# Linear attention on one core: exponentials of the next group before the scores, one tile per direction, and state steps between the groups

## The chip, the core and the metric

One core of a Trainium2 chip runs the whole program. Its engines work side by side, each through its own list of instructions: TensorE (PE in the rows; its weight loads are PEld), VectorE (DVE), ScalarE (ACT), GpSimd (POOL) and SyncE (SP), which issues the loads of weights from memory. The metric is the time of one execution in microseconds (us); it is given as the median of runs. A ratio is the changed kernel's time over the time of the kernel before.

## The reference

Two blocks run one after the other. The first is a trunk of two layers for two streams of 256 tokens, the context `cx` and the latents `x`. In each layer an input projection feeds three mixers: pooling, gated linear attention in both directions (four heads of 64), and softmax attention. Their results go through `w_out`, and a squared-ReLU MLP follows. The factors `sh`, `sc` and `ga` come from one row times `w_mod`. The second block, which the change doesn't touch, has a gated delta rule, dilated attention and two more MLPs.

```python
def gla_chunk_scan(q, k, v, la, s0, strict):
    ...
    mask = np.tril(np.ones((C, C), bool), k=-1 if strict else 0)[:, :, None]

    def step(S, inp):
        qc, kc, vc, lc = inp
        b = jnp.cumsum(lc, axis=2)
        o_inter = jnp.einsum('bhid,bhde->bhie', qc * jnp.exp(b), S)
        diff = b[:, :, :, None, :] - b[:, :, None, :, :]
        decay = jnp.exp(jnp.where(mask, diff, -jnp.inf))
        A = jnp.einsum('bhid,bhjd,bhijd->bhij', qc, kc, decay)
        o = o_inter + jnp.einsum('bhij,bhje->bhie', A, vc)
        bl = b[:, :, -1:, :]
        S_new = jnp.exp(bl[:, :, 0, :, None]) * S + jnp.einsum('bhjd,bhje->bhde', kc * jnp.exp(bl - b), vc)
        return S_new, o
    ...

def gla_bidir(q, k, v, la_f, la_b, s_f, s_b):
    o_f, s_f_new = gla_chunk_scan(q, k, v, la_f, s_f, strict=False)
    rev = lambda a: a[:, ::-1]
    o_b, s_b_new = gla_chunk_scan(rev(q), rev(k), rev(v), rev(la_b), s_b, strict=True)
    return o_f + rev(o_b), s_f_new, s_b_new

def trunk_layer(x, cx, c, c_ctx, ...):
    sh1, sc1, ga1, sh2, sc2, ga2 = modulation(c, w_mod, b_mod)
    ...
    u = (rmsnorm(x, g_mix) * (1 + sc1) + sh1) @ w_in
    uc = (rmsnorm(cx, g_mix) * (1 + sc1c) + sh1c) @ w_in
    ...
    o_gc, s_f, s_b = gla_bidir(*gla_features(gqc, gkc, gvc, rfc, rbc, w_gate, b_gate), s_zero, s_zero)
    o_gl, _, _ = gla_bidir(*gla_features(gq, gk, gv, rf, rb, w_gate, b_gate), s_f, s_b)
    ...
    mix = jnp.concatenate([pool_mixer(...), gla_output(o_gl, ...), latent_attention(ql, k_all, v_all)], axis=-1) @ w_out
    x = x + ga1 * mix
    x = x + ga2 * squared_relu_mlp(rmsnorm(x, g_mlp) * (1 + sc2) + sh2, w_up, w_down)
    ...
```

The latents' scan starts from the states that the context's scan leaves. In layer 1 the context needs only its states.

## The kernel before

The weight projections fill most of TensorE's time. `load_split` (L85) loads a 128x2x512 piece of weights into `raw` (three buffers), and ScalarE and VectorE split it into `hi` (L93) and `lo` (L94); each product is then three matmuls, hi by hi, hi by lo and lo by hi. The pieces of `w_mod` go from `raw` to TensorE without a split, as matmuls of 32x256 with `silu_c` (L407 loads them). Products land in PSUM tiles that belong to a thread: `ps_m` has three buffers, `ps_a` two, `ps_b` two and `ps_o` one. Linear attention works in thread a, and so never has more than two PSUM tiles. Softmax attention works in thread b.

Linear attention takes a stream's heads in pairs. `gla_pair` (L652) makes the decay logarithms `la` (as `la_h` and `la_l`), multiplies them by constant tables `cm` to get sums of logarithms, and takes the exponential on ScalarE (`gla_exp`, L608). Within 128 tokens `gla_intra` (L616) takes the decay between two rows in seven levels of block halves, of 64, 32, 16, 8, 4, 2 and 1 rows, two levels to a group and the last alone. For a group:

- 8 matmuls with `cm` (4 for each direction) make the logarithms, and two exponentials on ScalarE write the group's one tile `E`, which has one buffer for both directions;
- for each level four products on VectorE (L646), of a direction and a kind (q or k), write the tile `lev`;
- for each level four matmuls, each on half the rows of the array (64x128), make the scores of the two heads, head 0 in one `ps_a` tile and head 1 in another; in the trace each of the four is two records;
- two masked copies on VectorE (L649) put them into `at`.

Ahead of the levels stand the state steps (L662 to L685), four in a pair of the context and two in a pair of the latents. Each is a chain over three engines: product `qd` on VectorE (L667), transposition on TensorE (L669), copy `ktt` on ScalarE (L671), matmul on TensorE, and two small updates of the state on VectorE (L681, L683).

Six pairs go through `gla_intra`: two of the context in layer 0, two of the latents in each layer. Two more, of the context in layer 1, make states only.

When the program is built, a scheduler writes out each engine's order from the order of the code and from what each instruction needs; nothing is reordered at run time. Between the instructions of linear attention it puts others that are ready. In the context's two pairs of layer 0 these are matmuls of the input projection (128x512, called fillers in the text). Around the latents' pairs they are the 32x256 matmuls of the pieces of `w_mod` that stream in there, and softmax attention. `w_out` comes after that.

## Time and profile before

| | |
|---|---|
| three runs | 1900.25, 1903.61 and 1904.91 us; the median is 1903.61 us |
| the profiled execution | 1901.48 us, with a span of 1899.4 us inside it |
| mean granted clock of TensorE | 0.994 |
| TensorE busy | 1825.4 us, 96% of the span |
| VectorE, ScalarE busy | 1288.2 us (68%), 1068.3 us (56%) |
| DMA | 307.14 MB, 162 GB/s in the mean |

The span runs from the first instruction of the profiled execution to its last; the time of that execution is 2.1 us more. Busy times overlap between engines, so they don't add up. A matmul's end in a profile is modelled and matmuls are pipelined: the distance from one start to the next tells more than the printed duration.

### The profile page before, as it was taken

How to read it: one execution, taken by the hardware profiler on the slowest of the kernel's cores; microseconds unless marked ns; L12 is line 12 of the kernel's file. 1: busy time of each engine (PE TensorE's matmuls, PEld its weight loads, DVE VectorE, ACT ScalarE, POOL GpSimd, SP SyncE). 2: the span in 40 equal slices, each digit the busy share in tenths (PEclk: the TensorE clock that was granted, in tenths of full speed). 3: DMA queues.
4: the chain of work that ended last, by engine and by line, in shares of the span. 5: the costliest groups of instructions: out<-in, count | busy, mean ns of one | idle time of the engine just before them, and what ended most of it. 6: DMA issues, size and time to landing. Idle time of an engine off the chain costs nothing.

```text
span 1899.4 us, 33154 instructions
## 1 busy us (share of the span) xinstructions
PE 1825.4 (96%) x12272; PEld 1544.8 (81%) x12272; DVE 1288.2 (68%) x2853; ACT 1068.3 (56%) x2080; POOL 59.1 (3%) x60
## 2 busy tenths in 40 slices
PE   7998999999989999999899999998999999999999
PEld 5875567888879998856598889897899987789997
DVE  4465467677777767766566688777766677767665
ACT  5443647755575556646655557453554556675553
POOL 0000000000000000000000000403000000000000
PEclk9999999999999999999999999999999999999999
DMA  7414771355646565466256654131455654435665
GB/s 284 152 46 145 259 257 55 129 187 185 192 131 189 181 195 168 155 198 217 78 168 191 194 173 133 58 101 45 150 187 188 190 175 155 134 112 178 186 191 156
DMA packets 90225, 307.14 MB, mean 162 GB/s; under 512 B 11456, under 2 KB 16096, under 8 KB 90064
## 3 DMA queue, kind: packets, MB, share of 16 engines
q1 hardware_dynamic: 89088, 302.91, 50.1%
q0 software_dynamic: 976, 2.12, 0.3%
q8 instruction: 96, 1.57, 0.3%
q14 instruction: 65, 0.53, 0.1%
HBM read 303.95 MB, written 1.05 MB: 161 GB/s over the span
## 4 chain that ended last, share of the span: by engine, by line
PE 83%; DVE 7%; DMA 4%; ACT 4%; issue 2%; POOL 0%; DVEq 0%; ACTq 0%; POOLq 0%
PE ps_m L76 60%; PE ps_a L76 13%; PE ps_b L76 4%; PE ps_o L76 2%; DMA raw<-in_w_mod_dram 2%; ACT gt L296 1%; DVE k L1202 1%; DVE lo L94 1%; PE ps_b L834 1%; PE ps_b L1215 1%; ACT hh L244 1%; PE ps_m L288 1%; DMA tmpb<-in_band_dram 1%; DMA raw<-in_gdn_w_in_dram 0%; PE ps_m L415 0%
## 5 line engine op out<-in xcount | busy, mean ns | idle before, releaser
L93 ACT CAST hi<-raw 128x512 fp32r<-128x512 f32 (+1 forms) x944 | 576.7, 617 | 533.4 <-PE ps_m L76 288.7
L94 DVE TENSOR_TENSOR lo<-raw,hi 128x512 fp32r<-128x512 f32 (+1 forms) x944 | 636.1, 682 | 330.7 <-PE ps_m L76 203.4
L76 PE MATMUL ps_m<-hh,hi 128*128 128x256 f32 x1440 | 405.4, 282 | 8.9 <-ACT gt L296 4.3
L76 PE MATMUL ps_m<-hh,lo 128*128 128x256 f32 x1440 | 403.2, 281 | 3.9 <-DVE lo L94 3.9
L76 PE MATMUL ps_m<-hl,hi 128*128 128x256 f32 x1440 | 404.5, 281 | 0.0
L76 PE MATMUL ps_m<-hi,k 128*128 128x512 f32 x1120 | 352.0, 395 | 0.0
L76 PEld LDWEIGHTS ps_m<-hh,hi 128*128 128x128 f32 x1440 | 269.4, 187 | 14.9 <-ACT gt L296 6.4
L76 PEld LDWEIGHTS ps_m<-hh,lo 128*128 128x128 f32 x1440 | 268.9, 187 | 5.7 <-DVE lo L94 5.2
L76 PEld LDWEIGHTS ps_m<-hl,hi 128*128 128x128 f32 x1440 | 269.7, 187 | 2.4 <-issue 0.8
L76 PEld LDWEIGHTS ps_m<-hi,k 128*128 128x128 f32 x1120 | 208.5, 187 | 49.3
L76 PE MATMUL ps_m<-lo,k 128*128 128x512 f32 x560 | 221.2, 395 | 0.0
L76 PE MATMUL ps_m<-hi,hh 128*128 128x512 f32 (+1 forms) x440 | 175.0, 399 | 1.4 <-ACT hh L244 0.7
L76 PE MATMUL ps_m<-hi,hl 128*128 128x512 f32 (+1 forms) x440 | 172.0, 391 | 0.3 <-DVE hl L245 0.2
L76 PE MATMUL ps_m<-lo,hh 128*128 128x512 f32 (+1 forms) x440 | 171.7, 393 | 0.1
L76 PEld LDWEIGHTS ps_m<-lo,k 128*128 128x128 f32 x560 | 105.0, 187 | 25.6
L76 PE MATMUL ps_a<-hh,hi 128*128 128x256 f32 (+1 forms) x360 | 100.7, 280 | 0.0
L76 PE MATMUL ps_a<-hl,hi 128*128 128x256 f32 (+1 forms) x360 | 100.5, 279 | 0.0
L76 PE MATMUL ps_a<-hh,lo 128*128 128x256 f32 (+1 forms) x360 | 100.5, 279 | 0.0
L76 PEld LDWEIGHTS ps_m<-hi,hh 128*128 128x128 f32 x440 | 82.8, 188 | 20.9 <-ACT hh L244 1.3
L76 PEld LDWEIGHTS ps_m<-hi,hl 128*128 128x128 f32 x440 | 82.9, 188 | 17.6 <-issue 1.2
L76 PEld LDWEIGHTS ps_m<-lo,hh 128*128 128x128 f32 x440 | 82.6, 188 | 17.2 <-DVE lo L94 0.6
L76 PEld LDWEIGHTS ps_a<-hh,hi 128*128 128x128 f32 (+1 forms) x360 | 66.9, 186 | 0.5 <-ACT hh L249 0.2
(577 smaller groups left out, 2567.0 us busy)
## 6 DMA issues: line engine op xcount, KB each, us to landing
raw<-in_w_up_dram SPq DMA_DIRECT2D x96, 512.0 KB, 4.1
raw<-in_w_down_dram SPq DMA_DIRECT2D x96, 512.0 KB, 3.6
raw<-in_w_mod_dram SPq DMA_DIRECT2D x88, 512.0 KB, 4.4
raw<-in_ffn_w_in_dram SPq DMA_DIRECT2D x88, 512.0 KB, 3.5
raw<-in_ffn_w_out_dram SPq DMA_DIRECT2D x44, 512.0 KB, 3.5
raw<-in_dil_w_in_dram SPq DMA_DIRECT2D x36, 512.0 KB, 3.5
raw<-in_w_in_dram SPq DMA_DIRECT2D x32, 512.0 KB, 4.1
raw<-in_gdn_w_in_dram SPq DMA_DIRECT2D x32, 512.0 KB, 4.1
```

Of the source, the lines that this page charges most:

```text
L76: self.nc.tensor.matmul(out, lhsT, rhs, start=start, stop=stop)
L93: nc.scalar.copy(hi[:, c0:c1], raw[:, i, c0:c1])
L94: ins = nc.vector.tensor_sub(lo[:, c0:c1], raw[:, i, c0:c1], hi[:, c0:c1].bitcast(F32))
L244: self.nc.scalar.copy(hi, src)
L288: self.nc.tensor.transpose(ps[:, k * 256 + tt * 128:k * 256 + tt * 128 + 128], xs[tt][:, kt * 128:kt * 128 + 128], self.ident[:])
L296: self.nc.scalar.activation(f[:, k], src(k), AF.Identity, bias=sh[:, kt:kt + 1], scale=G[:, kt:kt + 1])
L834: nc.tensor.transpose(ps[:, kt * 128:kt * 128 + 128], p[:, kt * 128:kt * 128 + 128], self.ident[:])
L1202: nc.vector.scalar_tensor_tensor(y[:, sh:256], p[:, 0:256 - sh], w[:, 3 - sh:4 - sh], y[:, sh:256], op0=OP.mult, op1=OP.add)
L1215: self.nc.tensor.transpose(ps[:, h * 128:h * 128 + 128], src(h), self.ident[:])
```

## The change

Four things change in linear attention, and nothing elsewhere except one name.

1. `E` becomes a tile for each direction (two buffers in all), and the exponentials of the next group are written in the code after this group's products and before its scores.
2. The layout of `qk` and `E` is turned so that one product on VectorE covers both kinds, q and k, of a level and a direction: 84 products of 256 elements where there were 168 of 128.
3. The state steps go into `gla_intra` as `extras`: one after each group's scores. The arithmetic is the same.
4. At the start of the program, one of the first loads of `w_mod` borrows the tile `PT` in place of the old `E`.

```diff
@@ -500,7 +500,7 @@
 
         def done_qk(s, n, ps):
             which = n if full else 1
-            o = U[s]["qk"][:, :, :, which, :]
+            o = U[s]["qk"][:, :, which]
             i = ps[:].rearrange("p (f t c) -> p f t c", f=2, t=2)
             if which == 0:
                 nc.scalar.activation(o, i, AF.Copy, scale=0.125)
...
@@ -611,42 +611,61 @@
         for tt in range(2):
             for k in range(2):
                 self.mm(ps[:, tt * n:tt * n + n], la[k][:, tt, d, :], self.cm[d][:, c0:c0 + n], k == 0, k == 1)
-        self.nc.scalar.activation(out, ps[:, 0:2 * n].rearrange("p (t c) -> p t c", t=2), AF.Exp, scale=1.0 / 16.0)
-
-    def gla_intra(self, qk, la):
+        i = ps[:, 0:2 * n].rearrange("p (t c) -> p t c", t=2)
+        if len(out.shape) == 4:
+            i = i.rearrange("p t (l x) -> p t l x", x=out.shape[3])
+        self.nc.scalar.activation(out, i, AF.Exp, scale=1.0 / 16.0)
+
+    def gla_intra(self, qk, la, extras=()):
+
 
         nc = self.nc
         at = self.tile([128, 2, 2, 128], name="at", bufs=1)
+        extras = list(extras)
 
         def scores(L):
             pss = [self.ps() for _ in range(2)]
             for tt in range(2):
                 for h in range(2):
                     b = slice(64 * h, 64 * h + 64)
-                    self.mm(pss[h][:, tt * 128:tt * 128 + 128], L[b, tt, 1], L[b, tt, 0], True, True)
+                    self.mm(pss[h][:, tt * 128:tt * 128 + 128], L[b, 1, tt], L[b, 0, tt], True, True)
             return [ps[:, 0:256].rearrange("p (t c) -> p t c", t=2) for ps in pss]
 
-        for h, s in enumerate(scores(qk)):
-            nc.scalar.copy(at[:, h], s)
+        def exps(g):
+            n = 128 * len(LEVELS[2 * g:2 * g + 2])
+            Es = [self.tile([128, 512], name="E", bufs=2) for _ in range(2)]
+            for d in range(2):
+
+                self.gla_exp(la, d, 256 + 256 * g, n, Es[d][:, 0:2 * n].rearrange("p (l t x) -> p t l x", t=2, x=64))
+            return Es
+
+        def halves(t, d, s):
+
+            (ps, pn), (ws, wn), (ts, tn), (cs, cn) = t.ap
+            assert (wn, ts, tn, cs, cn) == (2, 128, 2, 1, 128)
+            return bass.AP(t.tensor, t.offset + (0 if d else s),
+                           [[ps, pn], [ws + (s if d else -s), 2], [2 * s, 128 // s], [1, s]])
+
+        Es = exps(0)
+        for h, sc in enumerate(scores(qk)):
+            nc.scalar.copy(at[:, h], sc)
         for g in range(4):
-            levels = LEVELS[2 * g:2 * g + 2]
-            n = 128 * len(levels)
-            E = self.tile([128, 2, 2, 256], name="E", bufs=1)
+            E = Es
+            Ls = [(s, self.tile([128, 2, 2, 128], name="lev", bufs=2)) for s in LEVELS[2 * g:2 * g + 2]]
             for d in range(2):
-                self.gla_exp(la, d, 256 + 256 * g, n, E[:, d, :, 0:n])
-            for li, s in enumerate(levels):
-                L = self.tile([128, 2, 2, 128], name="lev", bufs=2)
-                for d in range(2):
-                    for w in range(2):
-                        half = (1 - w) if d == 0 else w
-                        o = L[:, :, w].rearrange("p a (b h s) -> p a b h s", h=2, s=s)[:, :, :, half]
-                        i = qk[:, :, w].rearrange("p a (b h s) -> p a b h s", h=2, s=s)[:, :, :, half]
-                        e0 = li * 128 + w * 64
-                        e = E[:, d, :, e0:e0 + 64].rearrange("p a (b s) -> p a b s", s=s)
-                        nc.vector.tensor_tensor(o, i, e, OP.mult)
+                for li, (s, L) in enumerate(Ls):
+                    e = E[d][:, 256 * li:256 * li + 256].rearrange("p (w b x) -> p w b x", w=2, x=s)
+                    nc.vector.tensor_tensor(halves(L[:], d, s), halves(qk, d, s), e, OP.mult)
+            if g < 3:
+                Es = exps(g + 1)
+            for s, L in Ls:
                 m = self.xmask[:, LEVELS.index(s)].unsqueeze(1).to_broadcast([128, 2, 128])
                 for h, sc in enumerate(scores(L)):
                     nc.vector.copy_predicated(at[:, h], m, sc)
+            if extras:
+                extras.pop(0)()
+        for f in extras:
+            f()
         return at
...
+        def step(d, n, tt):
...
+        steps = [lambda d=d, n=n, tt=(d, 1 - d)[n]: step(d, n, tt) for n in range(2 if final else 1) for d in range(2)]
         if o is None:
+            for f in steps:
+                f()
             return
-        at = self.gla_intra(qk, la)
+        at = self.gla_intra(qk, la, steps)
...
-            first += [self.tile([128, 2, 2, 256], name=nm)[:].rearrange("p a b c -> p (a b) c") for nm in ("dec", "E")]
+            first.append(self.tile([128, 2, 2, 256], name="dec")[:].rearrange("p a b c -> p (a b) c"))
+            first.append(self.tile([128, 4, 2, 128], name="PT", bufs=2)[:].rearrange("p a b c -> p a (b c)"))
...
```

The body of `step` is the body of the old loop over state steps, unchanged but for the order of indices in `qk`.

How instructions move shows in the orders of three places. The first is TensorE's order in the first pair of the context, around the scores of the first group (levels 64 and 32). Before (`ps_a` tiles are linear attention's, `ps_m` and `ps_o` rows with `hi` and `lo` are fillers):

```order
L76 MATMUL ps_m_1435<-lo_1478,hh_186 128x512
L76 MATMUL ps_a_1058<-lev_1053 128x128
L76 MATMUL ps_a_1059<-lev_1053 128x128
L76 MATMUL ps_a_1058<-lev_1053 128x128
L76 MATMUL ps_a_1059<-lev_1053 128x128
L76 MATMUL ps_o_1436<-hi_1477,hh_186 128x512
L76 MATMUL ps_o_1436<-hi_1477,hl_187 128x512
L76 MATMUL ps_a_1071<-lev_1066 128x128 x2
L76 MATMUL ps_a_1072<-lev_1066 128x128 x2
L76 MATMUL ps_o_1436<-lo_1478,hh_186 128x512
L76 MATMUL ps_a_1080<-cm0_942,la_h_966 128x256
```

Now the same two levels:

```order
L76 MATMUL ps_a_1020<-cm1_949,la_l_967 128x256
L76 MATMUL ps_m_1414<-hi_1453,hl_185 128x512
L76 MATMUL ps_a_1026<-lev_1006 128x128 x2
L76 MATMUL ps_m_1414<-lo_1454,hh_184 128x512
L76 MATMUL ps_a_1027<-lev_1006 128x128 x2
L76 MATMUL ps_a_1034<-lev_1007 128x128 x2
L76 MATMUL ps_m_1415<-hi_1453,hh_186 128x512
L76 MATMUL ps_a_1035<-lev_1007 128x128 x2
L76 MATMUL ps_m_1415<-hi_1453,hl_187 128x512
L686 MATMUL ps_a_1044<-c_ident_69,qd_1042 128x128
L76 MATMUL ps_m_1415<-lo_1454,hh_186 128x512
```

The two heads' scores of a level were a block of four matmuls, with the heads taken in turn or one after the other. Now a filler stands between the heads of each level, and the next group's `cm` matmuls (the row of `ps_a_1020` is their last) and the transposition of a state step stand where they did not.

The second place is VectorE's order for the same group. Before:

```order
L646 TENSOR_TENSOR lev_1053<-k4_286,E_1040 128x2x64 x2
L646 TENSOR_TENSOR lev_1066<-k4_286,E_1040 128x2x2x32
L646 TENSOR_TENSOR lev_1053<-k4_286,E_1040 128x2x64 x2
L646 TENSOR_TENSOR lev_1066<-k4_286,E_1040 128x2x2x32 x3
L649 COPY_PREDICATED at_1031<-xmask_938,ps_a_1058 128x256
L649 COPY_PREDICATED at_1031<-xmask_938,ps_a_1059 128x256
L649 COPY_PREDICATED at_1031<-xmask_938,ps_a_1071 128x256
L649 COPY_PREDICATED at_1031<-xmask_938,ps_a_1072 128x256
```

Now:

```order
L684 TENSOR_TENSOR qd_1042<-k4_286,dec_970 128x128
L658 TENSOR_TENSOR lev_1006<-k4_286,E_984 128x2x2x64
L658 TENSOR_TENSOR lev_1007<-k4_286,E_984 128x2x4x32
L658 TENSOR_TENSOR lev_1006<-k4_286,E_985 128x2x2x64
L658 TENSOR_TENSOR lev_1007<-k4_286,E_985 128x2x4x32
L664 COPY_PREDICATED at_983<-xmask_938,ps_a_1026 128x256
L664 COPY_PREDICATED at_983<-xmask_938,ps_a_1027 128x256
L658 TENSOR_TENSOR lev_1054<-k4_286,E_1012 128x2x8x16
L664 COPY_PREDICATED at_983<-xmask_938,ps_a_1034 128x256
L658 TENSOR_TENSOR lev_1054<-k4_286,E_1013 128x2x8x16
L664 COPY_PREDICATED at_983<-xmask_938,ps_a_1035 128x256
```

Eight products became four, and the next group's products (`lev_1054`) stand between this group's masked copies.

The third place is TensorE's order in layer 1, in the latents' first pair, where the fillers run out and the second stretch of `w_mod` begins. Before, ahead of the first `w_mod` matmul (the row with `raw_9541`):

```order
L76 MATMUL ps_m_9449<-lo_9523,hh_8227 128x512
L76 MATMUL ps_m_9540<-raw_9541,silu_c_73 32x256
L76 MATMUL ps_a_9000<-lev_8995 128x128
L76 MATMUL ps_a_9001<-lev_8995 128x128
L76 MATMUL ps_a_9000<-lev_8995 128x128
L76 MATMUL ps_a_9001<-lev_8995 128x128
L76 MATMUL ps_m_9540<-raw_9541,silu_c_73 32x256 x3
```

Now (`raw_9481` is the same piece):

```order
L76 MATMUL ps_a_8996<-lev_8968 128x128 x2
L76 MATMUL ps_m_9389<-lo_9463,hh_8187 128x512
L686 MATMUL ps_a_9005<-c_ident_69,qd_9003 128x128
L76 MATMUL ps_m_9480<-raw_9481,silu_c_73 32x256 x4
L76 MATMUL ps_m_9480<-raw_9487,silu_c_73 32x256
L76 MATMUL ps_a_9009<-k4_8451,ktt_9007 128x128
```

Counted from the program's start, 418 matmuls of linear attention stood ahead of that first one, and now 441. The first matmul of `w_out` in layer 1 had 386 matmuls of softmax attention ahead of it and now has 406. In layer 0, 273 matmuls of linear attention and 188 of softmax attention stood ahead of `w_out`, and now 298 and 172. In the context's first pair TensorE's order held 74 fillers and now holds 53; in the second it held 80 and now 55. The loads on SP's queue keep their order but for a few that move by some places.

## Rows read from the trace of the kernel before

**Rows 1.** The page, parts 1 and 4: busy times and the last chain.

```profile
PE 1825.4 (96%) x12272; PEld 1544.8 (81%) x12272; DVE 1288.2 (68%) x2853; ACT 1068.3 (56%) x2080; POOL 59.1 (3%) x60
PE 83%; DVE 7%; DMA 4%; ACT 4%; issue 2%; POOL 0%; DVEq 0%; ACTq 0%; POOLq 0%
```

**Rows 2.** Busy time by stretch: stretch, length, engines, clock, DMA share, GB/s.

```profile
84.00:121.00 37.00, 36.80 (x214) 27.51 (x212) 22.09 (x70) 15.56 (x31) 0.00 (x0) 1.00 0.17 55
121.00:157.00 36.00, 35.80 (x211) 27.18 (x210) 23.46 (x77) 17.54 (x36) 0.00 (x0) 1.00 0.16 48
166.00:199.00 33.00, 27.11 (x230) 15.30 (x222) 15.12 (x44) 15.66 (x37) 2.15 (x4) 0.90 0.73 241
199.00:255.00 56.00, 51.61 (x480) 28.37 (x476) 34.03 (x130) 33.94 (x94) 0.54 (x1) 1.00 0.84 280
...
819.00:885.00 66.00, 62.03 (x561) 38.00 (x553) 45.63 (x163) 28.48 (x64) 2.15 (x4) 1.00 0.75 249
885.00:925.00 40.00, 36.56 (x215) 24.76 (x212) 23.05 (x50) 30.95 (x66) 0.00 (x0) 1.00 0.24 78
```

**Rows 3.** Waits of TensorE's weight loads, 84 to 158 us: total, times, longest.

```profile
PEld ps_a L76 <- DVE at L649: 3.5, 12, 0.4
PEld ps_a L76 <- issue: 3.4, 8, 0.5
PEld ps_a L76 <- ACT ktt L671: 2.2, 7, 0.4
PEld ps_a L669 <- DVE qd L667: 0.8, 2, 0.4
```

**Rows 4.** Timeline of PE near 98 us: start, duration, engine, line, operation.

```profile
98.35 0.40 PE L76 MATMUL ps_m<-lo,hh 128*128 128x512 f32 x1
98.68 0.71 PE L76 MATMUL ps_a<-k 64*128 64x128 f32 x4
99.32 0.38 PE L76 MATMUL ps_a<-cm,la_h 128*128 128x256 f32 x1
```

**Rows 5.** Timeline of PE, second group of the first pair, 106.5 to 109.8 us.

```profile
106.51 0.40 PE L76 MATMUL ps_m<-hi,hl 128*128 128x512 f32 x1
106.74 0.39 PE L76 MATMUL ps_m<-lo,hh 128*128 128x512 f32 x1
107.23 0.72 PE L76 MATMUL ps_a<-lev 64*128 64x128 f32 x8
107.88 0.50 PE L76 MATMUL ps_m<-hi,hh 128*128 128x512 f32 x1
108.21 0.39 PE L76 MATMUL ps_m<-hi,hl 128*128 128x512 f32 x1
108.53 0.95 PE L76 MATMUL ps_a<-lev 64*128 64x128 f32 x8
109.41 0.50 PE L76 MATMUL ps_m<-lo,hh 128*128 128x512 f32 x1
```

**Rows 6.** Timeline of DVE, same pair: the products of two groups.

```profile
100.72 1.71 DVE L646 TENSOR_TENSOR lev<-k,E 128x128 f32<-128x128 f32 x8 [2.59 <-ACT E L614]
...
105.98 1.71 DVE L646 TENSOR_TENSOR lev<-k,E 128x128 f32<-128x128 f32 x8 [0.61 <-ACT E L614]
```

**Rows 7.** Products on DVE by line, whole span: ns least/median/most, first and last start.

```profile
L646 DVE TENSOR_TENSOR lev<-k,E x112: 282/286/304, 100.7 to 871.0; 128x128 f32<-128x128 f32 x112
```

```profile
L245 DVE TENSOR_TENSOR hl<-gt,hh x56: 415/420/427, 22.3 to 947.6; 128x256 fp32r<-128x256 f32 x56
```

**Rows 8.** Timeline of SP: start of a row's first load, time to its last's, count.

```profile
166.46 88.06 SPq L407 DMA_DIRECT2D raw<-in_w_mod_dram  x45
```

```profile
199.25 30.17 SPq L407 DMA_DIRECT2D raw<-in_w_mod_dram  x17
```

```profile
819.29 61.59 SPq L407 DMA_DIRECT2D raw<-in_w_mod_dram  x29
```

**Rows 9.** Waits of TensorE's weight loads, 881 to 925 us: the largest.

```profile
PEld ps_b L834 <- ACT tmpb L819: 3.5, 7, 1.1
PEld ps_b L76 <- ACT PT L835: 1.7, 4, 0.8
```

More of the change, by code (lines that the diff above doesn't have):

```diff
@@ L489, in four @@
                 return self.k4() if streams[s] == l else self.tile([128, 1024], name="ux", bufs=4)
-            u["qk"] = four()[:].rearrange("p (a t w c) -> p a t w c", a=2, t=2, w=2)
+            u["qk"] = four()[:].rearrange("p (a w t c) -> p a w t c", a=2, t=2, w=2)
             g = four()
@@ L661, in gla_pair @@
         final = stream == CTX
-        for d in range(2):
-            for n, tt in enumerate((d, 1 - d)):
-                if n == 1 and not final:
-                    continue
-                kt = self.tile([128, 128], name="qd", bufs=1)
-                nc.vector.tensor_tensor(kt[:], qk[:, tt, 1], dec[:, d, tt, 128:256], OP.mult)
-                ps = self.ps()
-                nc.tensor.transpose(ps[:, 0:128], kt[:], self.ident[:])
-                ktt = self.tile([128, 128], name="ktt", bufs=1)
-                nc.scalar.copy(ktt[:], ps[:, 0:128])
-                ps = self.ps()
-                self.mm(ps[:, 0:128], ktt[:], gv[:, tt], True, True)
-                new = self.tile([128, 128], name=f"st{d}{n}{stream}" + (str(pair) if n else ""), bufs=1)
-                nc.vector.memset(new[:], 0.0)
-                old = state[d, n, pair]
-                col = 127 if d == 0 else 0
-                for half in range(2):
-                    b = slice(64 * half, 64 * half + 64)
-                    if old is None:
-                        nc.vector.tensor_copy(new[b, b], ps[b, b])
-                    else:
-                        nc.vector.scalar_tensor_tensor(new[b, b], old[b, b], dec[b, d, tt, col:col + 1], ps[b, b],
-                                                       op0=OP.mult, op1=OP.add)
-                state[d, n + 1, pair] = new
@@ new lines, in step @@
+        def step(d, n, tt):
+            kt = self.tile([128, 128], name="qd", bufs=1)
+            nc.vector.tensor_tensor(kt[:], qk[:, 1, tt], dec[:, d, tt, 128:256], OP.mult)
+            ps = self.ps()
+            nc.tensor.transpose(ps[:, 0:128], kt[:], self.ident[:])
+            ktt = self.tile([128, 128], name="ktt", bufs=1)
+            nc.scalar.copy(ktt[:], ps[:, 0:128])
+            ps = self.ps()
+            self.mm(ps[:, 0:128], ktt[:], gv[:, tt], True, True)
+            new = self.tile([128, 128], name=f"st{d}{n}{stream}" + (str(pair) if n else ""), bufs=1)
+            nc.vector.memset(new[:], 0.0)
+            old = state[d, n, pair]
+            col = 127 if d == 0 else 0
+            for half in range(2):
+                b = slice(64 * half, 64 * half + 64)
+                if old is None:
+                    nc.vector.tensor_copy(new[b, b], ps[b, b])
+                else:
+                    nc.vector.scalar_tensor_tensor(new[b, b], old[b, b], dec[b, d, tt, col:col + 1], ps[b, b],
+                                                   op0=OP.mult, op1=OP.add)
+            state[d, n + 1, pair] = new
@@ L694, in gla_pair @@
                     qd = self.tile([128, 128], name="qd", bufs=1)
-                    nc.vector.tensor_tensor(qd[:], qk[:, tt, 0], dec[:, d, tt, 0:128], OP.mult)
+                    nc.vector.tensor_tensor(qd[:], qk[:, 0, tt], dec[:, d, tt, 0:128], OP.mult)
                     jobs.append((tt * 128, 128, qd[:], st[:]))
@@ L704, in gla @@
     def gla(self, u, c, state, stream, want_out=True):
-        o = u["qk"][:, :, :, 0, :] if want_out else None
+        o = u["qk"][:, :, 0] if want_out else None
         for pair in range(2):
```

## The prediction

> **What bounds the kernel now.** I read the page first. TensorE is busy for 96% of the span and stands for 83% of the chain that ended last, VectorE for 7% [rows 1]. So a shorter VectorE instruction is worth nothing by itself. What counts is TensorE's work, its waits, and the places where something other than TensorE sets the pace.
>
> The stretches in which linear attention runs tell where that is, by their busy times [rows 2]. They are of three kinds:
>
> - In the context's two pairs (84 to 157 us) TensorE is busy for 36.80 of 37 us and 35.80 of 36 us. Fillers of the input projection close nearly every gap.
> - In the two stretches where `w_mod` streams in (166 to 255 us and 819 to 885 us) TensorE has idle time: 5.9 us in the first part, 4.4 us in the second and 4.0 us in layer 1. DMA is at 0.73, 0.84 and 0.75 there. In the second part it moves 280 GB/s, the most of all rows shown.
> - In layer 1 the end of softmax attention follows (885 to 925 us), with 36.56 of 40 us busy. Its weight loads wait for ScalarE, above all for `tmpb`, 3.5 us [rows 9].
>
> Then the waits of TensorE's weight loads in the context's pairs [rows 3]. The order can only touch those for a masked copy to free a `ps_a` tile (3.5 us), for `ktt` (2.2 us) and for `qd` (0.8 us), 6.5 us in all. The 3.4 us of issue have no releaser. VectorE waits for the exponential ahead of a group's products, 2.59 us in one group and 0.61 us in another [rows 6], but TensorE meanwhile runs fillers, so that this wait is hidden.
>
> **The change part by part.**
>
> *The merged products.* A product of 128 elements takes 286 ns, and one of 256, by the nearest row, a subtraction of the same width, 420 ns [rows 7]. 168 x 0.286 less 84 x 0.420 is 12.8 us less on VectorE over the six pairs. What hides it is TensorE's own queue: VectorE was the waiting side. Taken as 0; if the cover were gone, a group's scores would come 4 x (2 x 0.286 - 0.420) = 0.6 us sooner, which is part of the waits counted below.
>
> *The exponentials ahead and the steps between groups.* They add no matmul. The exponentials of the next group need a `ps_a` tile each, and only two exist, so the scores that follow take those same tiles once ScalarE has emptied them. The steps no longer run one behind the other with TensorE waiting for `ktt` and `qd`. Each has a group's scores, copies and next products around it. I take two thirds of the 6.5 us as gone, -4.3 us: the steps' 3.0 us should go nearly whole, but a masked copy still frees each `ps_a` tile. The bounds are 0, where a new wait takes their place, and -6.5 us.
>
> *The scores apart.* This is what the order shows and the diff doesn't say. A level's two heads, four matmuls in one block before, now have a filler between them. What a block costs is read from starts. Fillers follow each other by 0.23 us (106.51 to 106.74) [rows 5]. One head alone takes from the filler's start at 98.35 to the next work at 99.32, which is 0.97 us, so 0.74 us more than the filler [rows 4]. Both heads in turn take 106.74 to 107.88, 0.91 us more than the filler, and one head after the other 108.21 to 109.41, 0.97 us [rows 5]. The first filler behind a block takes 0.33 us, 0.10 more than the others. A group of two levels cost 0.91 + 0.97 + 2 x 0.10 = 2.08 us. Now it is one head, then the other head with the next level's first, then one head: 0.74 + 0.97 + 0.74 + 3 x 0.10 = 2.75 us. That is 0.67 us more in a group, and over four groups 2.7 us in a pair. As an upper bound I keep 2.7, as a lower one 0, since a filler placed inside may use a gap that stood elsewhere.
>
> The same rows show why the heads belong together: eight records with the heads in turn run from 107.23 to 107.88, 0.65 us, and four of one head run from 98.68 to 99.32, 0.64 us. The second head was free. The Trainium skill, "TensorEngine Tiling (Array Packing)", section "Key Properties", says that tiles operate independently and that a switch of tiling mode drains the engine. The trace agrees with the first by these two numbers, and the late start at 107.23 after a filler at 106.74 fits the second; by the rule each further block costs a drain on either side, which makes it the rule behind the slower rival below.
>
> Now stage by stage, where each part meets what bounds it:
>
> - *Context, layer 0.* TensorE is the bound, so the blocks count whole: 2 x 2.7 = +5.4 us, against -4.3 us of waits. Sum **+1.1 us** (-6.5 to +5.4). The pairs take 21 and 25 fillers fewer, but those still have to run, behind the pairs, and so they neither gain nor lose.
> - *First stretch of `w_mod`.* 45 loads follow each other by 88.06/44 = 2.00 us; the best run among them goes by 30.17/16 = 1.89 us [rows 8]. The loads' pace decides. The 2.7 us of the latents' first pair lie in the 4.4 us that TensorE idles there. **0**, between -5.0 us (all 44 distances at 1.886 us) and +2.7 us.
> - *Behind it.* 25 more matmuls of linear attention stand ahead of `w_out`, 16 of softmax attention fewer. A matmul in the context's stretch costs 36.80/214 = 0.17 us [rows 2], so nine more in the stretch that has idle time give **-1.5 us** (-4.3 to +2.7, by the 25 alone and by the second pair's blocks). The blocks and waits of that second pair I take as even, as they nearly are in the context.
> - *Layer 1.* The first `w_mod` matmul comes 23 matmuls later, +4.0 us. The stretch is relieved of these 23 and takes 20 of softmax attention, a net -0.5 us. The end behind it has 20 fewer, -3.4 us, and about 0.6 us of its waits for ScalarE with them. Sum **-0.5 us**. The bounds are -8.8 us, if the 29 loads (61.59/28 = 2.20 us apart [rows 8]) went at the pace of 1.886 us, and +5.4 us, if both pairs' blocks counted whole.
>
> The sum is 1.1 + 0 - 1.5 - 0.5 = -0.9 us against the profiled execution's 1901.48 us, so 1900.6 us. The median of the runs is 2.1 us higher, 1903.61 us, which gives 1902.7 us. Each split has as many small terms on the side of a gain, so I state 1902 us.
>
> **The rivals.**
>
> *Faster: the waits go and the loads go at their best pace.* The masked copies' wait goes with the steps' waits (-6.5 us), half of the blocks' price falls into gaps (+2.7 us), and TensorE frees `raw` soon enough that half of both stretches' slack is recovered: -2.5 and -4.4 us. With -1.5 us behind the first stretch that is -12.2 us, some 1891 us. For it speaks that a load takes 1.886 us in one part of a stretch and 2.00 or 2.20 us over the whole of it [rows 8], and that the chain of linear attention gets shorter. Against it: TensorE's queue takes linear attention and `w_mod` matmuls in a fixed order, and it is 92% to 94% busy in two of these stretches [rows 2].
>
> *Slower: the blocks count and the waits stay.* The scores stand apart in the context (+5.4 us), in the latents' second pair (+2.7 us), and in layer 1 with the 1.4 us that go beyond its 4.0 us of idle time: +9.5 us, some 1913 us. It decides from where less than a fifth of the 6.5 us of waits goes. For it speaks [rows 5]; against it, that the filler inside gives VectorE time to free the tile for the next scores.
>
> *The change doesn't do what it says.* The two `ps_a` tiles hold the next exponentials back until the masked copies of the level before are done, the filler inside pays for it, and what is shorter on VectorE stays hidden: within 1 us of 1903.6 us.
>
> **How the numbers follow.** The three runs spread from 1900.25 to 1904.91 us, 0.12% to either side; 0.3%, 5.7 us, is about what a measurement can tell from no change. I give my forecast 0.30, the change without effect 0.14, the faster rival 0.33 and the slower one 0.23. The first two end within 0.3%: 0.44. The range goes from a little below the faster rival, 1889 us, to just under the slower one's centre, 1912 us, and leaves 0.2 out. The likeliest two cases alone lie between 1898 and 1909 us.
>
> **What would show each step right or wrong.** In the changed kernel's profile VectorE should be busy for about 12.8 us less, and its wait for `E` nearly gone. The waits of weight loads for `ktt` and `qd` in the context's pairs should fall from 3.0 us to under 1 us, and those for `at` to half. A score block should stand as one head's four records with a filler behind it; if these take 0.64 us each, the +5.4 us are right, and if a filler overlaps with them they are too large. The loads' distances in the `w_mod` stretches should stay at 2.0 and 2.2 us. If they fall towards 1.89 us, the faster rival holds. If the stretch from 84 us to the first `w_mod` load gets longer by more than 4 us, the slower one does.

## The result

The changed kernel is slower: 1913.79 us in the median of ten runs, against 1904.87 us for the kernel before. The ratio is 1.0052, with a 95% interval of 1.0039 to 1.0065. I had forecast no change, 1902 us in a range that ended at 1912 us. The rival that I gave 0.23, split blocks that count while the waits stay, had named 1913 us.

The profile page of the changed kernel, its span and part 1, which answer to [rows 1]:

```profile
span 1908.4 us, 33069 instructions
PE 1836.7 (96%) x12272; PEld 1554.3 (81%) x12272; DVE 1280.3 (67%) x2769; ACT 1069.3 (56%) x2080; POOL 58.9 (3%) x60
```

TensorE ran the same 12272 matmuls and was busy for 11.3 us more, in a span that grew by 9.0 us. VectorE was busy for 7.9 us less. So TensorE became less efficient at the same work. A lower clock is not the reason: the mean granted clock was 0.996 in this execution and 0.994 in that of the kernel before. Over the changed kernel's ten runs it is 0.9945 in the mean; the kernel before had 0.991 to 0.992 in the series of the experiments below.

Busy time by stretch, with the columns of [rows 2]; the stretches with `w_mod` are moved by about as much as their start moved:

```profile
84.00:121.00 37.00, 36.67 (x202) 27.45 (x201) 20.10 (x54) 15.95 (x32) 0.00 (x0) 1.00 0.14 44
121.00:157.00 36.00, 35.67 (x196) 26.89 (x195) 24.34 (x70) 18.48 (x38) 0.00 (x0) 1.00 0.11 31
157.00:173.00 16.00, 16.00 (x79) 12.53 (x81) 3.12 (x7) 3.08 (x6) 0.00 (x0) 1.00 0.20 67
173.00:206.00 33.00, 28.06 (x256) 16.45 (x248) 16.16 (x47) 19.74 (x47) 2.14 (x4) 1.00 0.81 270
206.00:262.00 56.00, 52.93 (x465) 29.91 (x464) 32.48 (x114) 32.48 (x86) 0.00 (x0) 1.00 0.83 266
```

Between 84 and 157 us TensorE is as full as before, but with 202 and 196 matmuls where there were 214 and 211. The fillers that the pairs no longer took stand behind them, alone, from 157 to 173 us.

The `w_mod` stretches on SP's queue, with the columns of [rows 8]; first the 45 loads of layer 0, then all 32 of layer 1:

```profile
173.21 87.15 SPq L407 DMA_DIRECT2D raw<-in_w_mod_dram  x45
```

```profile
806.10 88.48 SPq L407 DMA_DIRECT2D raw<-in_w_mod_dram  x32
```

Layer 1's 32 loads in the kernel before:

```profile
801.63 79.25 SPq L407 DMA_DIRECT2D raw<-in_w_mod_dram  x32
```

The first stretch began at 166.46 us and lasted 88.06 us; now it begins 6.8 us later and lasts 87.15 us. Layer 1's 32 loads began at 801.63 us and took 79.25 us before; now they take 9.2 us more.

Followed by counting the same TensorE matmuls in both traces, the delay grows like this: 0.6 us at the first pair's start (`cm` matmul at 91.00 us), 6.7 us at the first `w_mod` matmul (172.51 us), 7.0 us at the first load of `w_out`, 3.9 us in layer 0's up projection, 4.2 us in layer 1's input projection, 9.9 us in its MLP, and 9.0 us at the end. So there are two places of loss: the context's pairs (+6.2 us) and layer 1 (+5.7 us). Behind the first `w_mod` stretch 3.1 us come back. Not all of that is the change's: in the trace of the kernel before, TensorE's granted clock was 0.57 for four microseconds there, and in the changed kernel's it was 1.00 from 262 to 400 us. At half the clock, 3.4 us of full work cost up to 1.7 us (an estimate).

```profile
298.00:302.00 4.00, 3.52 (x17) 3.52 (x18) 3.07 (x11) 4.00 (x11) 0.00 (x0) 0.57 0.01 2
```

What the block of scores costs stands in the timeline of TensorE, first group of the first pair; it answers to [rows 5]:

```profile
97.15 0.39 PE L76 MATMUL ps_m<-hi,hl 128*128 128x512 f32 x1
97.52 0.71 PE L76 MATMUL ps_a<-lev 64*128 64x128 f32 x4
98.16 0.49 PE L76 MATMUL ps_m<-lo,hh 128*128 128x512 f32 x1
98.58 0.96 PE L76 MATMUL ps_a<-lev 64*128 64x128 f32 x8
99.47 0.50 PE L76 MATMUL ps_m<-hi,hh 128*128 128x512 f32 x1
99.90 0.71 PE L76 MATMUL ps_a<-lev 64*128 64x128 f32 x4
100.53 0.50 PE L76 MATMUL ps_m<-hi,hl 128*128 128x512 f32 x1
```

One head's four records take 0.64 us, from 97.52 to 98.16, as long as eight took with the heads in turn [rows 5]. From the filler at 97.15 to the one at 100.53 are 3.38 us; three fillers of 0.23 us in it leave 2.7 us for the group, and the last filler's longer pace adds 0.1 us. That is 2.8 us, close to the 2.75 us that I had worked out.

And the waits of TensorE's weight loads, 84 to 158 us, the largest, which answer to [rows 3]:

```profile
PEld ps_a L76 <- ACT ktt L688: 2.4, 7, 0.4
PEld ps_a L76 <- issue: 2.3, 8, 0.4
PEld ps_a L76 <- DVE at L664: 1.8, 6, 0.4
PEld ps_a L76 <- ACT E L617: 1.4, 5, 0.3
PEld ps_a L76 <- PE ps_a L76: 1.2, 4, 0.4
PEld ps_a L76 <- ACT dec L617: 0.6, 2, 0.3
```

The wait for the masked copies halved and the one for `qd` is gone from the list. `ktt` is as large as before, and waits that did not exist came in, for the exponentials to empty a `ps_a` tile. The three waits named in the prediction went from 6.5 us to 4.2 us, and these new ones (`E`, `dec` and a `ps_a` predecessor) are 3.2 us. The waits without a releaser (issue) went from 3.4 us to 2.3 us.

### The profile page after: what moved, and what is told of

It is laid out like the page before. It is cut to its first block, busy times and chain, and to the rows that moved or that the text cites. A ratio compares the mean times of both kernels' runs of the same rounds, so it can differ in the third digit from the quotient of the medians.

```text
span 1908.4 us, 33069 instructions
## 1 busy us (share of the span) xinstructions
PE 1836.7 (96%) x12272; PEld 1554.3 (81%) x12272; DVE 1280.3 (67%) x2769; ACT 1069.3 (56%) x2080; POOL 58.9 (3%) x60
## 4 chain that ended last, share of the span: by engine, by line
PE 84%; DVE 6%; ACT 4%; DMA 3%; issue 3%; POOL 0%; DVEq 0%; ACTq 0%; POOLq 0%; SPq 0%
PE ps_m L76 60%; PE ps_a L76 14%; PE ps_b L76 4%; PE ps_o L76 3%; DMA raw<-in_w_mod_dram 2%; ACT gt L296 1%; DVE k L1223 1%; PE ps_b L854 1%; DVE lo L94 1%; DMA tmpb<-in_band_dram 1%; PE ps_m L288 1%; ACT hh L244 1%; PE ps_b L1236 1%; DMA raw<-in_gdn_w_in_dram 0%; PE ps_a L1236 0%
## 5 line engine op out<-in xcount | busy, mean ns | idle before, releaser
L76 PEld LDWEIGHTS ps_a<-hl,hi 128*128 128x128 f32 (+1 forms) x360 | 66.9, 186 | 0.4 <-DVE hl L250 0.2
```

The lines of the kernel that those rows point to most:

```text
L76: self.nc.tensor.matmul(out, lhsT, rhs, start=start, stop=stop)
```

## The experiments

Two theories stood against each other. Theory S: the split blocks cost the time. Rival W: the moves cost it, by new waits or by what they put ahead of the `w_mod` stretches. All ratios are to the kernel before, run in turn on the same chip; all intervals are 95%. The series were taken on four chips, so that kernels of different series are compared by their ratios. Delays by place are of one profiled execution each and so less sure than the ratios: the run "before, together" ended 4.6 us late in its profile while its median is 1.3 us below that of the kernel before. Part of this is the granted clock, which differs between executions of one kernel; where it bears on a delay, it stands beside it.

**Heads together.** Why is a level's block split at all? Because the two heads' tiles come free at different times. One way to that: ahead of the scores now stand the exponentials, which use both `ps_a` tiles. ScalarE empties the first one exponential earlier than the second, so head 0 is ready sooner than head 1, and the scheduler puts a filler between. The edit keeps the whole change and makes head 0 wait until head 1's tile is free too. `self.read` is the last instruction that reads the latest `ps_a` tile; it is set at each exponential, copy and state update.

```diff
+    def after_it(self, ins, other):
+        self.tc.add_manual_dep(ins.ins, other.ins.name, mybir.DependencyInfo(
+            mybir.DependencyClass.Sync, mybir.DependencyReason.ANTI), reason="both heads' tiles")
...
-                    self.mm(pss[h][:, tt * 128:tt * 128 + 128], L[b, 1, tt], L[b, 0, tt], True, True)
+                    ins = self.mm(pss[h][:, tt * 128:tt * 128 + 128], L[b, 1, tt], L[b, 0, tt], True, True)
+                    if h == 0:
+                        self.after_it(ins, self.read)
```

> The changed kernel, but each score matmul of head 0 is also made to follow the instruction that empties head 1's PSUM tile, so that the four matmuls of a level stand as one block with the heads in turn (63 blocks on TensorE's order instead of 86; 64 before). Theory S (the split blocks cost the time): the context's pairs get back about 0.7 us per group, some 6 us, the first w_mod matmul comes at about 167 us again instead of 174, and the whole lands near the kernel before, 1902 to 1907 us. Rival W (the moved exponentials and steps cost it, by new waits or by the work that they put ahead of the w_mod stretches): blocks in one piece wait longer for their second tile, and the time stays at 1911 to 1916 us.

Measured: 1900.83 us, ratio 0.9975 (0.9962 to 0.9989). TensorE's busy time fell to 1818.7 us, 18.0 us below the changed kernel's and 6.7 us below that of before. Its timeline, around the first group:

```profile
96.61 0.40 PE L76 MATMUL ps_o<-lo,hh 128*128 128x512 f32 x1
96.93 0.72 PE L76 MATMUL ps_a<-lev 64*128 64x128 f32 x8
97.58 0.50 PE L76 MATMUL ps_m<-hi,hh 128*128 128x512 f32 x1
97.92 0.40 PE L76 MATMUL ps_m<-hi,hl 128*128 128x512 f32 x1
98.15 0.40 PE L76 MATMUL ps_m<-lo,hh 128*128 128x512 f32 x1
98.38 0.40 PE L76 MATMUL ps_m<-hi,hh 128*128 128x512 f32 x1
98.71 0.71 PE L76 MATMUL ps_a<-lev 64*128 64x128 f32 x8
99.35 0.50 PE L76 MATMUL ps_m<-hi,hl 128*128 128x512 f32 x1
```

Each block goes from the filler's start to the next work in 0.97 us (96.61 to 97.58, and 98.38 to 99.35), and the filler behind it takes 0.34 us, so a block costs 0.84 us and a group 1.7 us, 1.1 us less than split. The named waits of the weight loads (84 to 164 us) didn't fall with it; on the contrary:

```profile
PEld ps_a L76 <- ACT E L622: 2.9, 8, 0.4
PEld ps_a L76 <- ACT ktt L695: 2.9, 8, 0.4
PEld ps_a L693 <- DVE at L671: 2.4, 8, 0.3
PEld ps_a L76 <- DVE at L671: 2.2, 6, 0.4
```

So the time came back with more named waits, not fewer (the rows above of the changed kernel end at 158 us; its pairs end at 152 us). Rival W falls, and theory S holds; it even undersold the edit, which lands below its range and beats the kernel before.

**The parts of the change, one by one.** Three kernels undo the moves singly or both, without the tie.

```diff
-            if g < 3:
-                Es = exps(g + 1)
             for s, L in Ls:
...
+            if g < 3:
+                Es = exps(g + 1)
             if extras:
```

> The changed kernel with the next group's exponentials written behind the scores again; merged products, tiles per direction and steps between the groups stay. 80 blocks. Theory S, at (1913.8 - 1904.9)/(86 - 64) = 0.4 us a block: about 1911 us. A theory that the exponentials ahead cost the time: like the kernel before, 1903 to 1907 us. One that the steps between the groups cost it: like the changed kernel, 1912 to 1916 us.

Measured: 1909.18 us, ratio 1.0027 (1.0012 to 1.0042).

```diff
+        for f in steps:
+            f()
         if o is None:
-            for f in steps:
-                f()
             return
-        at = self.gla_intra(qk, la, steps)
+        at = self.gla_intra(qk, la)
```

> The changed kernel with all state steps ahead of the levels again; exponentials ahead and merged products stay. 76 blocks. Theory S at 0.4 us a block: about 1909.7 us. Exponentials as the cause: like the changed kernel, 1912 to 1916 us. Steps as the cause: 1903 to 1907 us.

Measured: 1913.76 us, ratio 1.0049 (1.0031 to 1.0068).

Both edits together:

> Only the merged products and the tiles of exponentials per direction; exponentials behind the scores and steps ahead of the levels as in the kernel before. 70 blocks. Theory S at 0.4 us a block: about 1907 us. If only the moves cost anything: 1903 to 1907 us, with the context's pairs as long as in the kernel before. If the merged products themselves cost time (a layout that is slower to read): above 1909 us, and their rows on VectorE well over 420 ns.

Measured: 1907.31 us, ratio 1.0015 (0.9998 to 1.0032). A count of blocks alone was too simple: with 76 blocks the run with the steps first is as slow as the changed kernel with 86, and by its median slower than the run with 80. Part of the first is the clock: these three kernels ran at a mean granted clock of 0.990 to 0.991, as did the kernel before beside them, and the changed kernel at 0.9945. In the 34 runs of the kernel before in this series, 0.001 of mean clock goes with 1.1 us, so that at their clock the changed kernel would take some 4 us more (an estimate). Without the tie, moving the exponentials seems to cost more than moving the steps, as the two ratios near 1.005 both have them ahead, though the intervals of 1.0049 and 1.0027 overlap. The counts also say that the exponentials are not the main thing that splits blocks: of the 22 blocks that the change adds, 6 go with the exponentials behind, 10 with the steps first, and 6 stay with the merged products alone. The merged products alone show no difference that this can tell from none.

**The same cuts with the tie.** If whole blocks were the one thing that mattered, the tie should help the kernel before too, and the moves should be equal.

> The kernel before with nothing but the same tie between the heads' score matmuls (62 blocks, all with the heads in turn, where 14 had one head after the other and 8 were single heads). Theory S prices this at 14 x 0.06 + 8 x 0.3, some 2 to 3 us, of which part lies in stretches with idle time: 1902 to 1905 us. If the tie itself, and not the change, made the run with the heads together fast, it lands at 1898 to 1902 us as well. If holding head 0 back costs a wait where nothing else is ready: above 1907 us.

Measured: 1902.87 us, ratio 0.9989 (0.9973 to 1.0005). The tie alone on the old order brings little or nothing.

The opposite, blocks made worse in the kernel before, and nothing else:

```diff
-            for tt in range(2):
-                for h in range(2):
+            for h in range(2):
+                for tt in range(2):
                     b = slice(64 * h, 64 * h + 64)
-                    self.mm(pss[h][:, tt * 128:tt * 128 + 128], L[b, tt, 1], L[b, tt, 0], True, True)
+                    ins = self.mm(pss[h][:, tt * 128:tt * 128 + 128], L[b, tt, 1], L[b, tt, 0], True, True)
+                    if h == 1 and tt == 0:
+                        self.behind(ins, last)
+                    last = ins
```

> The kernel before with the heads taken one after the other instead of in turn, and head 1 tied behind head 0: 70 blocks, 34 of them one head after the other (14 before). Theory S: 6 more blocks at 0.4 us and 20 more at 0.06 us, so 3 to 4 us more, 1907 to 1910 us. If blocks matter only together with the exponentials ahead: 1903 to 1907 us.

Measured: 1907.21 us, ratio 1.0019 (1.0007 to 1.0031). Worse blocks cost time without any of the change's moves, though little: this kernel's mean granted clock was 0.991 against 0.992 beside it, which may account for some 1 us of the 3 us.

> Merged products and tiles per direction only, with the tie between the heads. Theory S, by which a block in one piece costs the same in each: near the run with the heads together, 1899 to 1904 us. If the exponentials ahead and the steps between give a gain once the blocks are whole: 1904 to 1908 us, above that run by 3 us or more.

Measured: 1902.27 us, ratio 0.9995 (0.9985 to 1.0006). It lies above the run with the heads together by 0.0020, with intervals that overlap (0.9985 to 1.0006 and 0.9962 to 0.9989), so that a gain of the two moves is likely but not shown by this pair.

> The changed kernel with the state steps ahead of the levels again and the tie between the heads. If the steps between the groups bring something when the blocks are whole: 1903 to 1907 us, slower than the run with the heads together (1900.8). If they bring nothing: 1898 to 1903 us.

Measured: 1894.17 us, ratio 0.9954 (0.9937 to 0.9970). This is the fastest kernel of the study. Against merged, together, which was taken in the same series and differs in the exponentials alone, the intervals lie apart, so that whole blocks let the exponentials ahead pay. Some 2 us of the 8 us between the two may be the clock, 0.9935 against 0.9920 in the mean. I had expected the steps between the groups to bring something or nothing; here the run without them is the faster one, though the intervals of 0.9975 and 0.9954 overlap.

> The changed kernel with the next exponentials behind the scores again and the tie everywhere; steps stay between the groups. It completes the four: neither 0.9995 of the kernel before, exponentials ahead alone 0.9954, both 0.9975. If the two moves add up: 0.9995 + 0.0021 = 1.0016, some 1907 us. If the steps cost something only where the exponentials stand ahead: 0.999 to 1.000, 1902 to 1904 us.

Measured: 1900.01 us, ratio 0.9983 (0.9966 to 1.0000). With whole blocks, then, exponentials ahead alone give 0.9954, both moves 0.9975, steps between alone 0.9983, neither 0.9995. The run itself, 1900.01 us, lies below both of its expectations. Of the four only 0.9954 and 0.9995 have intervals apart, so that of the two moves the exponentials ahead alone are shown to be useful with whole blocks; without the tie they stand at 1.0049.

> The run with exponentials ahead, state steps first and the tie, but with four products a level again instead of two. If the merged products do nothing, since VectorE's time is hidden: 1892 to 1897 us. If they shorten the chain of a group by the 0.6 us that the prediction named, and the exponentials ahead need that: 1897 to 1904 us.

This kernel makes the four products of the old form from the new tiles, with the tie, exponentials ahead and steps first. Measured: 1898.80 us, ratio 0.9974 (0.9960 to 0.9988), inside the second expectation, but its interval overlaps that of 0.9954. What the merged products bring there stays open.

**Where the blocks count.** The context's two pairs hold 128 of the small records in every kernel. Their cost is the distance from the start of the matmul ahead of a block to the start of the next one behind it, less that matmul's own pace (0.23, 0.12 or 0.11 us by its width), plus what the next one takes over its pace; a matmul that stands between two blocks is counted once. A wait at the edge of a block is in it. The length is that from the first `cm` matmul of the first pair to the first `w_mod` matmul, so that it holds all fillers. For the changed kernel the first two of these rows of TensorE's timeline give 172.51 - 91.00 = 81.5 us; for the kernel before the other two give 165.76 - 90.43 = 75.3 us:

```profile
91.00 0.40 PE L76 MATMUL ps_a<-cm,la_h 128*128 128x256 f32 x2
```

```profile
172.51 0.64 PE L76 MATMUL ps_m<-raw,silu_c 128*32 128x256 f32 x8
```

```profile
90.43 0.28 PE L76 MATMUL ps_a<-cm,la_h 128*128 128x256 f32 x1
```

```profile
165.76 0.42 PE L76 MATMUL ps_m<-raw,silu_c 128*32 128x256 f32 x4
```

| kernel | blocks | their cost, us | length, us |
|---|---|---|---|
| changed | 26 | 23.1 | 81.5 |
| exponentials behind | 24 | 21.6 | 79.4 |
| steps first | 22 | 21.3 | 79.8 |
| before, split | 18 | 18.4 | 76.0 |
| before | 18 | 17.6 | 75.3 |
| merged only | 17 | 16.8 | 74.7 |
| before, together | 16 | 14.4 | 72.9 |
| merged, together | 16 | 14.1 | 72.5 |
| steps between, together | 16 | 13.6 | 72.3 |
| changed, together | 16 | 13.6 | 72.6 |
| ahead, steps first, together | 16 | 13.6 | 71.4 |

From bottom to top the cost rises by 9.5 us and the length by 10.1 us. The length less the cost is 57.6 to 59.0 us in every kernel. Here TensorE has nothing but work, so the blocks count one for one.

**By place.** The tie switched on for some pairs only, on the changed kernel (`self.tie` is set in `gla_pair` and tested where the tie is made).

```diff
-                    if h == 0:
+                    if h == 0 and self.tie:
...
+        self.tie = c["layer"] == 0 and stream == CTX
```

> The changed kernel with the tie between the heads only in the context's two pairs of layer 0 (75 blocks). Theory S with the places read from the traces: the entry into the first w_mod stretch comes 10 us sooner than in the changed kernel, layer 0 ends 4 to 11 us sooner, and the loss of layer 1, some 6 us, stays: 1903 to 1909 us. If the loss of layer 1 were only a late start handed on from layer 0: 1899 to 1903 us, like the tie everywhere.

Measured: 1906.71 us, ratio 1.0017 (1.0000 to 1.0034). The length above is 72.6 us, as with the tie everywhere. Layer 0 as a whole ends only 1.6 us sooner than in the changed kernel, less than expected: between the first `w_mod` matmuls and the first load of `w_out` 5.0 us of the gain go. The latents' pairs lie there, with their blocks still split as in the changed kernel. But this profiled execution is 4.3 us above its kernel's median, and its granted clock there was 0.94, against 1.00 in the changed kernel:

```profile
173.00:262.00 89.00, 81.44 (x699) 49.05 (x691) 46.90 (x152) 49.54 (x127) 2.45 (x5) 0.94 0.80 252
```

```profile
173.00:262.00 89.00, 80.99 (x719) 46.36 (x711) 48.65 (x161) 52.22 (x132) 2.14 (x4) 1.00 0.82 267
```

By that the clock alone may account for the 5.0 us; no run separates the two. And layer 1 still loses: its delay against the kernel before grows from 2.6 us in the input projection to 10.9 us in the MLP. Of these 8.3 us up to 3.4 us may be the clock, which was 0.69 from 878 to 889 us; in the kernel before and the changed kernel it was 1.00 there.

```profile
878.00:889.00 11.00, 9.26 (x70) 5.17 (x74) 2.96 (x8) 1.76 (x3) 0.54 (x1) 0.69 0.69 222
```

> The changed kernel with the tie only in layer 1 (79 blocks). Theory S by place: layer 0 as in the changed kernel, 4 us behind the kernel before at its end, and layer 1 adds 0 to 1 us: 1907 to 1911 us. If blocks cost nothing where w_mod streams in: 1912 to 1916 us.

Measured: 1911.08 us, ratio 1.0030 (1.0017 to 1.0043), a little above the expected time and with the parts as expected: the context's length stays 81.5 us, and layer 1 adds 0.5 us (3.7 to 4.2 us). So a tie in the context leaves layer 1's loss, and a tie in layer 1 leaves the context's.

What makes layer 1's loss was then still open: the late start of its `w_mod` stretch, or the blocks inside. In the first pair the tie takes 19 of linear attention's matmuls from ahead of the stretch; the second pair lies inside it.

> The changed kernel with the tie only in the latents' first pair of layer 1, the one that runs into the start of the w_mod stretch. On TensorE's order 19 matmuls of linear attention fewer stand ahead of the stretch. If layer 1's loss is the late start: nearly all of the tie in layer 1 comes back, layer 1 loses under 2 us, 1908 to 1912 us. If it is the blocks inside the stretch: layer 1 still loses 3 us or more, 1911 to 1915 us.

Measured: 1912.24 us, ratio 1.0037 (1.0023 to 1.0051). The stretch began early, but layer 1 still lost 4.6 us (from 4.4 us to 9.0 us).

> The changed kernel with the tie only in the latents' second pair of layer 1, which lies inside the stretch; the start of the stretch stays where the changed kernel has it. If layer 1's loss is the late start: 1912 to 1916 us as in the changed kernel, with layer 1 losing 5 us or more. If it is the blocks inside: 1908 to 1911 us.

Measured: 1914.45 us, ratio 1.0050 (1.0037 to 1.0064); layer 1 lost 6.0 us (6.3 to 12.3 us). The 32 loads of layer 1 on SP's queue, in the runs with the tie in layer 1, in the first pair and in the second pair:

```profile
805.48 79.87 SPq L412 DMA_DIRECT2D raw<-in_w_mod_dram  x32
```

```profile
805.85 84.86 SPq L412 DMA_DIRECT2D raw<-in_w_mod_dram  x32
```

```profile
807.65 87.56 SPq L412 DMA_DIRECT2D raw<-in_w_mod_dram  x32
```

Against the changed kernel's 88.48 us, the first pair saves 3.6 us, the second 0.9 us, and both 8.6 us. So neither theory holds alone: by these traces either pair's tie by itself gives little back, and both together nearly all. The two traces of the changed kernel with the tie in both pairs agree: 0.5 us lost with the tie in layer 1 alone, 0.3 us with the tie everywhere. The single pairs are one execution each, and their ratios, 1.0037 and 1.0050, have intervals that overlap with each other and with the changed kernel's. So that whole blocks in both pairs take the loss away is shown; how it divides between start and inside is open.

## Why the prediction was wrong

**The steps that failed** are two, the context's sum and layer 1's, which stands further down. In the context's sum, +1.1 us, it is the term of -4.3 us for waits that go. The stretch grew by 6.2 us, beyond the upper bound of +5.4 us. The price of the blocks was right: the first group costs 2.8 us split where I had worked out 2.75, and the two pairs together 5.5 us more than before, where I had +5.4. The waits gave nothing back; 0.7 us came on top. I had assigned them two thirds of 6.5 us because the steps no longer run back to back. But two `ps_a` tiles serve all of linear attention, and the named waits of 6.5 us became 4.2 us with 3.2 us of new ones. The prediction's own sign for the slower rival came true: the first `w_mod` load came 6.8 us later, more than 4 us.

**Merged products at nothing:** right within what can be measured without the tie (1.0015, 0.9998 to 1.0032). As durations they came out as sized; the 84 products show 411 to 432 ns and 404 to 427 ns:

```profile
L658 DVE TENSOR_TENSOR lev<-k,E x56: 411/418/432, 94.3 to 868.0; 128x256 f32<-128x256 f32 x56
L658 DVE TENSOR_TENSOR lev<-ux,E x28: 404/416/427, 192.8 to 309.3; 128x256 f32<-128x256 f32 x28
```

But VectorE as a whole fell by 7.9 us, not by the 12.8 us forecast. The forecast added up printed durations, and these overlap: eight old products in a row took 1.71 us [rows 6], 0.21 us each and not 0.286. A new one is followed 0.33 us after its start, not 0.42 us:

```profile
100.07 0.44 DVE L664 COPY_PREDICATED at<-xmask,ps_a 128x256 f32<-128x256 uint8 x1
100.40 0.42 DVE L658 TENSOR_TENSOR lev<-k,E 128x256 f32<-128x256 f32 x1
100.73 0.44 DVE L664 COPY_PREDICATED at<-xmask,ps_a 128x256 f32<-128x256 uint8 x1
101.07 0.42 DVE L658 TENSOR_TENSOR lev<-k,E 128x256 f32<-128x256 f32 x1
```

By these distances 168 x 0.21 less 84 x 0.33 is 7.6 us (an estimate), about what was measured.

**VectorE's wait for `E`:** it fell, but from 24.2 us to 9.8 us over the whole run, not to nearly nothing, and this was no gain, as the prediction said of a hidden wait.

**The first `w_mod` stretch:** 0 forecast, -0.9 us measured for its 45 loads. They kept their pace, 87.15/44 = 1.98 us from one to the next.

**Behind it:** -1.5 us forecast, -3.1 us measured. The direction is right, but up to 1.7 us of it is the low clock in the trace of the kernel before.

**Layer 1:** -0.5 us forecast, +5.7 us measured, just past the upper bound of +5.4. The start of the stretch came later by 11.0 us less the 4.2 us handed on, 6.8 us, where I had 4.0 us; I had priced the 23 matmuls ahead of it as if none of their blocks were split, which may be why. The step that failed here is the term that the sum put at nothing: I took the pairs' blocks as covered by idle time, since 4.0 us of it stood in the rows. The ties show that they are not: with whole blocks in both pairs the loss is 0.5 us.

**The chances.** The slower rival's own account, +5.4 in the context and the rest behind, gave 1913 us; its condition, that less than a fifth of the waits goes, is what the trace shows in the sum. That its total is so near is partly luck: it had +2.7 us in layer 0's latents, where 3.1 us came back, and +1.4 us in layer 1, where 5.7 us were lost. What the context shows agrees with it: a block costs 0.84 us whole, and each of the two halves of a split one about as much. The rule of the Trainium skill, "TensorEngine Tiling (Array Packing)", section "Key Properties", that a switch of tiling mode drains the engine and that tiles operate independently, was the rule behind this rival; these numbers fit it, though no run here separates a drain from other costs at a block's edge. I gave this rival 0.23, because I expected a filler inside a block to use a gap that stood elsewhere. In the changed kernel no such gap existed: TensorE was as full as before with fewer matmuls done.

## What to carry to other kernels

Where the engine that sets the end is full, look in the order at what it does, not only at what it waits for: the same matmuls in another arrangement cost 18 us of busy time here. Matmuls that share the array, one on each half of its rows, did best next to each other; if a scheduler splits them because their output tiles come free at different times, try tying both to the later one. With that tie the change's main idea, exponentials ahead of the scores, pays: with the state steps left ahead it stands at 0.9954, and without the tie at 1.0049. On the old order the tie alone showed no gain clear of noise (0.9989, 0.9973 to 1.0005).

## What the runs showed of the hardware

Four records on one half of the array's rows take 0.64 us, in the kernel before as in the changed one. Eight records with both halves in turn take 0.65 us, in the kernel before and in the run with the heads together. One half after the other, in one block of eight, takes 0.88 to 0.89 us. A block of either kind starts 0.09 us or more later behind a full-width matmul than the next full-width one would (0.09 us at 96.93, 0.14 us at 97.52, 0.26 us at 107.23), and the matmul behind it takes 0.33 us instead of 0.23 us. I had not expected that a wait added on purpose for half of the score matmuls would make the program 0.8% faster (0.9975 against 1.0052).

The granted clock is not the same in all executions of a kernel: the 34 runs of the kernel before in the first series have means of 0.987 to 0.995, and the lower go with the longer times. In its profiled execution the clock was at half, 1.2 GHz, from 186 to 192 us, while from 84 to 157 us it was at its full 2.4 GHz. So a delay of a few microseconds between two single executions has to be read with the clock of its stretch beside it.
